# Two expert blocks taken whole ahead of the register loads, and the end of the mix and the router taken token tile by token tile

## The chip, the cores and the metric

The kernel runs on one core of a Trainium2 chip. The metric is device time in microseconds (us), the median of several runs. Weights and activations are float32; TensorE multiplies them with the weights split into a high and a low part.

## The reference, cut to what matters

Two layers, 256 tokens, width 1024. Each adds a mixing sum to x and then a feed-forward sum; in the second layer that is two of eight experts per token.

```python
for l in range(DEPTH):
    h = rms_norm(x, mix_norm_g[l])
    ...
    x = x + jnp.concatenate([ya, yb, yc], axis=-1) @ w_out[l]
    h = rms_norm(x, ffn_norm_g[l])
    if l % 2 == 0:
        x = x + swiglu(h, dense_w_gate[i], dense_w_up[i], dense_w_down[i])
    else:
        x = x + moe_swiglu(h, moe_router[i], moe_w_gate[i], moe_w_up[i], moe_w_down[i])

def moe_swiglu(h, router, wg, wu, wd):
    logits = (t @ router).astype(jnp.float32)
    top_v, top_i = lax.top_k(logits, TOP_K)          # 2 of 8
    gates = jax.nn.softmax(top_v, axis=-1)
    ...
    for e in range(N_EXPERTS):                       # FF width 3584
        out = out + gate_full[:, e:e + 1] * swiglu(t, wg[e], wu[e], wd[e])
```

## The kernel before, in words

`mix(0)`, a dense feed-forward, `mix(1)` and `experts()` follow each other. A tile scheduler sets the order of the instructions on each engine from the order in which they are written, their priorities and its own estimate of their times; `tc.issue_after` pins one instruction behind another.

**End of the mix.** W_out is applied in matmuls of three terms (L201 to L203: high part, low part, low part of the input). Its four sums (two token tiles t of 128 tokens, two halves) stay in PSUM (`acc`) and are added to `x` on VectorE at L452, at the end of `mix`.

**Router.** For each token tile, eight 128x128 transposes of `x` (L1142, in two groups of four), a copy of each group to `xT` by ScalarE (L1143), eight matmuls with the router's weights (L1145) and the two largest logits (L1147, L1148). Then `xn = x*gain` (L1150), its high part `xh` (L1151, ScalarE), the indices as floats `ixf` (L1154), the one-hots `best` and `sel` (L1156, L1158), and the low part `xl` (L1160): tile 0 on VectorE, tile 1 on GpSimd. Three matmuls with `sel` (L1163 to L1165) rank the tokens of each expert; `slot_e` (L1168) is each token's place, from which the gathering one-hots `pe` are made (L1196). A second chain (L1306 to L1320) sorts the experts by their number of tokens into `order`.

**Experts.** Places p = 0 to 7 stand for experts. Place 0 is expert 0, whatever the routing; for the others the expert's number is read from `order` into a register on the SP engine (L1178, a TENSOR_LOAD). A place takes its tokens in a kind: QUARTER (32 places, matmuls L1486), NARROW (64) or WIDE (128; its weights are split into `wh` by ScalarE, L196, and `wl` by VectorE, L197). An expert has 7 blocks of 512 hidden columns; a block is six loads of 1 MB (four for gate and up, j = 0 to 3, two for down, j = 4 and 5), 336 in all. The SP queue issues them (`eload`; L1114 for expert 0, L1116 for an expert in a register). There are 12 load buffers, so load n waits until load n - 12 has been read. A load is taken as two halves.

`halves()` (L1402) lists the halves in the order of use: first the gate and up loads of the two lead blocks (LEAD = 2, both of expert 0, kind QUARTER), then the first wide block W0 and so on; the down loads of the lead blocks follow W0's. `fill` (L1420) draws up to WINDOW = 10 halves ahead; `take` (L1427) hands one out. `work()` (L1546) makes the up parts of the two lead blocks (`small_up`), then loops over the wide blocks: `wide_up` (L1434), W0's extra QUARTER part (`quarter_up`, which reads the same loads again and so frees them), transposition of the activations (`small_T`: L1510, copied by ScalarE at L1513; `wide_T`: L1497, L1500), `wide_down` of the block before, and `small_down` (L1539) of the small blocks taken in the turn before. In the first turn that is the down part of the lead blocks, behind `wide_up` of W0. Gathers of tokens are L1250 (small kinds, `xgs`) and L1264 (wide), followed by small matmuls for the norm and the scatter (L1204, L1215, L1217).

Of the kernel before, what the change touches and what calls it, by code (L numbers as in the profile page):

```python
# [13 lines left out]
F32 = mybir.dt.float32  # L14
# [115 lines left out]
def trunk(ctx: ExitStack, tc: tile.TileContext, x_in, pos_in, wst, moe, pp_in, rr_in, sw_in, rt_in,  # L130
# [163 lines left out]
    def mix(l):  # L294
# [805 lines left out]
    def experts():  # L1100
# [22 lines left out]
        def sml(name, shape, dt=F32):  # L1123
# [5 lines left out]
                        P(1, "ffng")[:, :, None].to_broadcast([128, KD, NE]), op=ALU.mult)  # L1129
        xT = big.tile([128, 2, KD, 128], F32, name="xT", tag="xg", bufs=2)  # L1130
        xn = big.tile([128, 2, DM], F32, name="xn", tag="xg", bufs=2)
        xh = big.tile([128, 2, DM], F32R, name="xh", tag="xh")
        xl = big.tile([128, 2, DM], F32R, name="xl", tag="xl")
        mx = sml("mx", [128, 2, 8])
        ix = sml("ix", [128, 2, 8], U32)
        for t in range(2):
            psl = pb()
            for g in range(2):
                ps = pa()
                for k in range(4):  # L1140
                    ks = slice((4 * g + k) * 128, (4 * g + k + 1) * 128)
                    T.transpose(ps[:, k * 128:(k + 1) * 128], x[:, t, ks], ident)  # L1142
                act(xT[:, t, 4 * g:4 * g + 4, :], ps.rearrange("p (k s) -> p k s", k=4), AF.Copy)  # L1143
# [9 lines left out]
        ixf = sml("ixf", [128, 2, 2])  # L1153
        V.tensor_copy(ixf, ix[:, :, 0:2])  # L1154
# [265 lines left out]
        def fill(n=0):  # L1420
            while len(feed) < WINDOW and sum(h[0] is not None for h in feed) <= AHEAD + n:
# [123 lines left out]

        def work():  # L1546
            m, wjob = LEAD, None
            before = [(np_, ni, small_up(np_)) for np_, ni in narrows[:LEAD]]
            drain()
            ask(NARROWS[1])  # L1550
            for n in range(len(wides) + 1):
# [25 lines left out]
                for (np_, ni, _), z in zip(before, nT):  # L1577
                    kind = KINDS[np_][0]
                    if ni == 0:
                        accs[np_] = [pa()[:, 0:512 if kind == NARROW else 256]]  # L1580
                    small_down(accs[np_][0], kind, ni, z, [take()[2] for _ in range(4)])
                    if ni == NB - 1:
                        ended(np_, kind, accs[np_], np_ == NARROWS[-1])
# [80 lines left out]
        with tc.issue_after(held_v.ins), tc.issue_after(held_a.ins):  # L1664
            fill(0)
# [9 lines left out]
    mix(0)  # L1675
    nc.sync.dma_start(rt, rt_in[:, 0:64])
    if stop != "mix0":
        ffn()
        if stop != "ffn":
            mix(1)  # L1680
            if stop != "mix1":
                experts()
# [145 lines left out]
```

## Time and profile before

| | us |
|---|---|
| median of 3 runs | 1416.01 (1412.99 to 1417.02) |
| the profiled execution's own time | 1414.25 |
| its span in the trace | 1412.5 |

| engine | busy us | share of the span |
|---|---|---|
| PE (matmul) | 1330.2 | 94% |
| DVE | 715.0 | 51% |
| ACT | 629.0 | 45% |
| POOL | 77.9 | 6% |

DMA moves 422.64 MB. The page shows the span in 40 slices of 35.3 us: the `experts` part begins in the sixteenth, where the DMA moves 71 GB/s, and from the eighteenth on it moves 340 to 427 GB/s in nearly every slice. A busy share near 100% over a long span can hide short stages with another limit, so the stages are read one by one in the rows below.

### The profile page before, as it was taken

How to read it: one execution, taken by the hardware profiler on the slowest of the kernel's cores; microseconds unless marked ns; L12 is line 12 of the kernel's file. 1: busy time of each engine (PE TensorE's matmuls, PEld its weight loads, DVE VectorE, ACT ScalarE, POOL GpSimd, SP SyncE). 2: the span in 40 equal slices, each digit the busy share in tenths (PEclk: the TensorE clock that was granted, in tenths of full speed). 3: DMA queues.
4: the chain of work that ended last, by engine and by line, in shares of the span. 5: the costliest groups of instructions: out<-in, count | busy, mean ns of one | idle time of the engine just before them, and what ended most of it. 6: DMA issues, size and time to landing. Idle time of an engine off the chain costs nothing.

```text
span 1412.5 us, 24089 instructions
## 1 busy us (share of the span) xinstructions
PE 1330.2 (94%) x9860; PEld 965.4 (68%) x9860; DVE 715.0 (51%) x1052; ACT 629.0 (45%) x986; POOL 77.9 (6%) x127
## 2 busy tenths in 40 slices
PE   7989899999999898998999999999999999999986
PEld 7977678888888676765666555655766656656553
DVE  5686455445576555453335314524544446565443
ACT  7548264444575643453224313423434345444342
POOL 1250000000114111000000000000000000000000
PEclk9989999999999997999999999999999999999989
DMA  7410245555452231899999999989999999999995
GB/s 285 178 61 2 90 153 185 189 188 179 159 185 74 84 159 71 337 425 425 425 427 425 426 385 374 426 372 426 402 426 413 420 427 426 426 411 426 427 426 226
DMA packets 60438, 422.64 MB, mean 299 GB/s; under 512 B 7200, under 2 KB 8224, under 8 KB 10400
## 3 DMA queue, kind: packets, MB, share of 16 engines
q1 hardware_dynamic: 59760, 420.03, 73.1%
q8 instruction: 79, 1.29, 0.3%
q10 hardware_dynamic: 560, 1.00, 0.2%
q14 instruction: 39, 0.32, 0.1%
HBM read 419.95 MB, written 1.05 MB: 298 GB/s over the span
## 4 chain that ended last, share of the span: by engine, by line
PE 76%; DMA 10%; DVE 6%; ACT 3%; POOL 2%; issue 2%; SPq 0%; ACTq 0%; DVEq 0%; POOLq 0%
PE pb L1470 10%; DMA raw<-moe 10%; PE pb L202 8%; PE pb L201 7%; PE pb L203 7%; PE pa L1539 7%; PE pa L202 6%; PE pa L201 6%; PE pa L203 6%; PE pb L1486 4%; DVE wl L197 2%; PE pb L1250 1%; PE pa L371 1%; PE pa L373 1%; PE pa L372 1%
## 5 line engine op out<-in xcount | busy, mean ns | idle before, releaser
L197 DVE TENSOR_TENSOR wl<-raw,wh 128x1024 fp32r<-128x1024 f32 (+1 forms) x370 | 440.8, 1221 | 180.1 <-ACT wh L196 179.4
L196 ACT ACTIVATE wh<-raw 128x1024 fp32r<-128x1024 f32 (+1 forms) x370 | 380.5, 1053 | 230.8 <-PE pb L203 118.4
L202 PE MATMUL pb<-wl,xg 128*128 128x512 f32 x336 | 141.3, 420 | 13.2 <-DVE wl L197 12.4
L1470 PE MATMUL pb<-raw,xgs 128*64 128x256 f32 x1344 | 151.0, 380 | 0.0
L201 PE MATMUL pb<-wh,xg 128*128 128x512 f32 x336 | 136.7, 409 | 9.9 <-ACT wh L196 9.9
L203 PE MATMUL pb<-wh,xg 128*128 128x512 f32 x336 | 134.0, 399 | 0.0
L1470 PEld LDWEIGHTS pb<-raw,xgs 128*64 128x64 f32 x1344 | 95.0, 137 | 54.7 <-issue 9.3
L1539 PE MATMUL pa<-raw,aT 128*32 128x256 f32 (+1 forms) x1008 | 120.1, 454 | 0.0
L1486 PE MATMUL pb<-raw,xgs 128*32 128x256 f32 x1344 | 93.1, 395 | 10.1 <-DMA raw<-moe 10.1
L202 PEld LDWEIGHTS pb<-wl,xg 128*128 128x128 f32 x336 | 64.4, 192 | 41.9 <-DVE wl L197 25.9
L1473 ACT ACTIVATE a<-pb,rg 128x256 f32<-128x256 f32 x21 | 9.9, 473 | 174.9 <-PE pb L1470 174.9
L1501 DVE TENSOR_TENSOR aT<-pb,aT 128x512 fp32r<-128x512 f32 x21 | 14.5, 692 | 143.7 <-ACT aT L1500 143.7
L201 PEld LDWEIGHTS pb<-wh,xg 128*128 128x128 f32 x336 | 64.2, 191 | 32.1 <-ACT wh L196 18.2
L1539 PEld LDWEIGHTS pa<-raw,aT 128*32 128x32 f32 (+1 forms) x1008 | 42.8, 118 | 61.9 <-issue 46.2
L1486 PEld LDWEIGHTS pb<-raw,xgs 128*32 128x32 f32 x1344 | 45.2, 113 | 50.9 <-DMA raw<-moe 14.1
L202 PE MATMUL pb<-wl,hTh 128*128 128x512 f32 (+1 forms) x192 | 73.0, 380 | 0.0
L203 PEld LDWEIGHTS pb<-wh,xg 128*128 128x128 f32 x336 | 64.5, 192 | 12.1
L203 PE MATMUL pb<-wh,hTl 128*128 128x512 f32 (+1 forms) x192 | 71.6, 377 | 0.0
L202 PE MATMUL pa<-wl,aT 128*128 128x512 f32 x168 | 69.0, 411 | 0.5 <-DVE wl L197 0.5
L201 PE MATMUL pb<-wh,hTh 128*128 128x512 f32 (+1 forms) x192 | 67.5, 378 | 0.7 <-ACT hTh L284 0.7
L203 PE MATMUL pa<-wh,aT 128*128 128x512 f32 x168 | 66.5, 396 | 0.0
L1475 DVE SCALAR_TENSOR_TENSOR a<-pb,rg,a 128x256 f32<-128x256 f32 x21 | 10.2, 484 | 99.4 <-PE pb L1470 99.4
(384 smaller groups left out, 2058.0 us busy)
## 6 DMA issues: line engine op xcount, KB each, us to landing
raw<-moe SPq DMA_DIRECT2D x336, 1024.0 KB, 12.3
raw<-wst SPq DMA_DIRECT2D x54, 1024.0 KB, 4.8
raw<-wst SPq DMA_DIRECT2D x4, 832.0 KB, 5.1
area<-sw_in SPq DMA_DIRECT2D x2, 960.0 KB, 7.1
area<-sw_in SPq DMA_DIRECT2D x2, 664.0 KB, 6.2
x<-x_in SPq DMA_DIRECT2D x2, 512.0 KB, 5.1
raw<-wst SPq DMA_DIRECT2D x2, 512.0 KB, 7.0
out_dram<-x SPq DMA_DIRECT2D x8, 128.0 KB, 2.7
```

The lines of the kernel that those rows point to most:

```text
L196: act(h[:, 0:n], t[:, a:b], AF.Copy)
L197: (E or V).tensor_tensor(lo[:, 0:n], t[:, a:b], h[:, 0:n].bitcast(F32), op=ALU.subtract)
L201: T.matmul(o, lhsT=xh, rhs=wh, start=first, stop=False)
L202: T.matmul(o, lhsT=xh, rhs=wl, start=False, stop=False)
L203: T.matmul(o, lhsT=xl, rhs=wh, start=False, stop=last)
L371: T.matmul(ps, lhsT=wh[:, s_], rhs=hTh[:, k, :], start=(k == 0), stop=False)
L372: T.matmul(ps, lhsT=wh[:, s_], rhs=hTl[:, k, :], start=False, stop=False)
L373: T.matmul(ps, lhsT=wl[:, s_], rhs=hTh[:, k, :], start=False, stop=(k == KD - 1))
L1470: T.matmul(ps[HALF[hv], :], lhsT=z[:, k, :], rhs=w[:, o_:o_ + 256], start=(k == 0), stop=(k == KD - 1))
L1486: T.matmul(ps[QUART[g], :], lhsT=z[:, k, :], rhs=ws[g // 2 * 4 + k // 2][:, o_:o_ + 256], start=(k == 0), stop=(k == KD - 1))
L1501: V.tensor_tensor(z[:, :, 1, :], p3, z[:, :, 0, :].bitcast(F32), op=ALU.subtract)
L1539: T.matmul(acc[rows, :], lhsT=aT[:, f, :], rhs=ws[f][:, g * w:g * w + w], start=(i == 0 and f == 0), stop=(i == NB - 1 and f == 3))
```

## The change

It has four parts.

- `mix()` returns its sums; `add_to_x` adds them per token tile, in `experts` within the router's loop, tile 1 behind `diff(0)`, the low part `xl` of tile 0.
- The router is written tile by tile: transposes go into the PSUM pool `pb` instead of `pa`; `xn`, `xh`, `ixf` and `xl` are made per tile; `xh` of tile 1 stands behind the last `xT` copy, `xl` of tile 1 moves from GpSimd to VectorE, behind `sel`.
- `halves()` lists all 12 loads of the two lead blocks first (gate and up of both, then down of both), and the first `fill` may draw 24 halves, so that all 12 are issued before the register loads.
- `work()` takes the two lead blocks whole (up, transposition, down) before the loop over the wide blocks.

```diff
-        for t in range(2):
-            for nh in range(2):
-                s_ = slice(nh * 512, nh * 512 + 512)
-                V.tensor_tensor(x[:, t, s_], x[:, t, s_], acc[2 * t + nh], op=ALU.add)
-        tap(f"xm{l}", x)
+        return acc
+
+    def add_to_x(acc, t):
+        for nh in range(2):
+            s_ = slice(nh * 512, nh * 512 + 512)
+            V.tensor_tensor(x[:, t, s_], x[:, t, s_], acc[2 * t + nh], op=ALU.add)
...
+        def diff(t):
+            return V.tensor_tensor(xl[:, t, :], xn[:, t, :], xh[:, t, :].bitcast(F32), op=ALU.subtract)
+
+        first = None
         for t in range(2):
+            with tc.issue_after(first.ins) if t else ExitStack():
+                add_to_x(mixed, t)
             psl = pb()
             for g in range(2):
-                ps = pa()
+                ps = pb()
...
+            V.tensor_tensor(xn[:, t, :], x[:, t, :], gr, op=ALU.mult)
 
             V.max(mx[:, t, :], psl[:, 0:NE])
             V.max_index(ix[:, t, :], mx[:, t, :], psl[:, 0:NE])
-        for t in range(2):
-            V.tensor_tensor(xn[:, t, :], x[:, t, :], gr, op=ALU.mult)
-            held_a = act(xh[:, t, :], xn[:, t, :], AF.Copy)
+            V.tensor_copy(ixf[:, t, :], ix[:, t, 0:2])
+            with tc.issue_after(last_T.ins) if t else ExitStack():
+                held_a = act(xh[:, t, :], xn[:, t, :], AF.Copy)
+            if t == 0:
+                first = diff(0)
...
-        V.tensor_tensor(sel, best[:, :, 0, :], best[:, :, 1, :], op=ALU.add)
-        for t, E in enumerate((V, G)):
-            E.tensor_tensor(xl[:, t, :], xn[:, t, :], xh[:, t, :].bitcast(F32), op=ALU.subtract)
+        chosen = V.tensor_tensor(sel, best[:, :, 0, :], best[:, :, 1, :], op=ALU.add)
+        with tc.issue_after(chosen.ins):
+            diff(1)
...
         def halves():
-            m, before = LEAD, narrows[:LEAD]
-            for b in before:
-                yield from units(*b, range(4))
+            m, before = LEAD, []
+            for js in (range(4), (4, 5)):
+                for b in narrows[:LEAD]:
+                    yield from units(*b, js)
...
         def work():
-            m, wjob = LEAD, None
-            before = [(np_, ni, small_up(np_)) for np_, ni in narrows[:LEAD]]
+            m, before, wjob = LEAD, [], None
+            lead = [(np_, ni, small_up(np_)) for np_, ni in narrows[:LEAD]]
+            small_downs(lead, [small_T(a_, KINDS[np_][0], NARROW) for np_, _, a_ in lead])
             drain()
...
         with tc.issue_after(held_v.ins), tc.issue_after(held_a.ins):
-            fill(0)
+            fill(0, 12 * LEAD)
```

In the instruction streams it shows at three places. Line numbers of the changed kernel lie some lines higher than those of the kernel before.

**The SP queue where the expert loads begin.** Before: eight loads of expert 0, then the first read of `order`, and between the reads the four gate and up loads of W0, whose expert is in a register.

```order
L1114 DMA raw<-moe 128x2048 x8
L1178 TENSOR_LOAD order
L1178 ISA x2
L1116 ISA
L1116 DMA raw<-moe 128x2048
L1178 TENSOR_LOAD order
...
L1594 TENSOR_LOAD flag_i
L1594 ISA x2
L1114 DMA raw<-moe 128x2048 x12
```

After:

```order
L1115 DMA raw<-moe 128x2048 x12
L1189 TENSOR_LOAD order
L1189 ISA x2
...
L1610 TENSOR_LOAD flag_i
L1610 ISA x2
L1117 ISA
L1117 DMA raw<-moe 128x2048
...
L1115 DMA raw<-moe 128x2048 x8
```

Four more loads stand ahead of the register loads, all eight reads stand together behind them, and W0's first load is now the thirteenth load instead of the ninth, so that it needs a buffer that one of the first twelve has left.

**PE at the end of W_out and in the router.** Before, all eight transposes of tile 0 (L1142, x8 higher up in the stream) stand among the last matmuls of W_out; behind these:

```order
L202 MATMUL pa<-wl,hTh 128x512
L203 MATMUL pa<-wh,hTl 128x512
L1142 MATMUL pa<-cc,x 128x128 x4
L1145 MATMUL pb<-rtg,xT 128x8 x4
L1142 MATMUL pa<-cc,x 128x128 x4
L1145 MATMUL pb<-rtg,xT 128x8 x12
L1163 MATMUL pb<-sel,cc 128x8
```

After:

```order
L202 MATMUL pa<-wl,hTh 128x512
L203 MATMUL pa<-wh,hTl 128x512
L1154 MATMUL pb<-rtg,xT 128x8 x4
L1151 MATMUL pb<-cc,x 128x128 x4
L1154 MATMUL pb<-rtg,xT 128x8 x4
L1151 MATMUL pb<-cc,x 128x128 x4
L1154 MATMUL pb<-rtg,xT 128x8 x4
L1151 MATMUL pb<-cc,x 128x128 x4
L1154 MATMUL pb<-rtg,xT 128x8 x4
L1174 MATMUL pb<-sel,cc 128x8
```

Only four transposes stand among W_out's matmuls now; three groups stand behind it, and each group of transposes alternates with the logits of the group before.

**ACT and PE at the lead blocks.** `a` is the silu of a block, `aT` its transposed copy, `wh` a split of W0's loads. ACT before:

```order
L196 ACTIVATE wh<-raw 128x1024 x2
L1488 ACT_TABLE_LOAD
L1488 ACTIVATE a<-pb,rg 64x256 x2
L1269 ACTIVATE xg<-pb 128x256
L1272 ACTIVATE xgs<-pb 128x32
```

ACT after:

```order
L1500 ACT_TABLE_LOAD
L1500 ACTIVATE a<-pb,rg 64x256
L196 ACTIVATE wh<-raw 128x1024 x3
L1500 ACTIVATE a<-pb,rg 64x256
L196 ACTIVATE wh<-raw 128x1024
L1525 ACTIVATE aT<-pb 128x2x2x32 x2
L1280 ACTIVATE xg<-pb 128x256
```

PE before:

```order
L1486 MATMUL pb<-raw,xgs 32x256 x63
L1264 MATMUL pb<-pe,xh 128x160 x2
L1264 MATMUL pb<-pe,xl 128x160 x2
```

PE after:

```order
L1498 MATMUL pb<-raw,xgs 32x256 x63
L1522 MATMUL pb<-cc,a 128x64 x2
L1551 MATMUL pa<-raw,aT 32x256 x15
L1522 MATMUL pb<-cc,a 128x64 x2
L1551 MATMUL pa<-raw,aT 32x256
L1275 MATMUL pb<-pe,xh 128x160 x2
```

The down parts of the lead blocks (L1551) stand directly behind their up parts on PE, and on ACT their `aT` copies stand behind four splits of W0's first two loads.

## Rows read from the trace of the kernel before

**Rows 1.** Stages: us, engines' busy us (x), PEclk granted, DMA share, GB/s.

```profile
600.00:660.00 60.00, 52.80 (x555) 36.13 (x549) 23.30 (x29) 23.71 (x34) 0.00 (x0) 0.95 1.01 425
660.00:820.00 160.00, 157.95 (x1236) 100.10 (x1235) 67.30 (x78) 57.87 (x76) 0.00 (x0) 1.00 1.01 424
820.00:1010.00 190.00, 187.10 (x1190) 117.69 (x1190) 75.82 (x90) 64.68 (x83) 0.00 (x0) 1.00 0.96 399
1010.00:1260.00 250.00, 243.23 (x1469) 160.66 (x1466) 122.17 (x133) 107.41 (x131) 0.00 (x0) 1.00 1.01 419
```

**Rows 2.** The same view in short stretches around the change.

```profile
530.00:540.00 10.00, 7.01 (x38) 4.49 (x38) 5.68 (x11) 2.43 (x4) 1.54 (x2) 1.00 0.00 0
...
550.00:555.00 5.00, 2.64 (x12) 2.55 (x12) 2.78 (x11) 1.68 (x6) 2.28 (x4) 0.50 0.01 2
...
610.00:620.00 10.00, 8.34 (x40) 6.92 (x37) 6.99 (x7) 7.82 (x10) 0.00 (x0) 0.83 1.01 427
```

**Rows 3.** SP queue's waits, 400 to 720 us: total, times, longest.

```profile
SPq L1178 <- DVE oh L1320: 45.0, 1, 45.0
```

**Rows 4.** Timeline of SP: start, us, instructions.

```profile
557.34 2.74 SPq L1116 DMA_DIRECT2D raw<-moe  x4
566.84 30.48 SPq L1114 DMA_DIRECT2D raw<-moe  x12
598.39 4.71 SPq L1116 DMA_DIRECT2D raw<-moe  x6
```

**Rows 5.** Issue at 557.3 us (W0's first load): median us to landing.

```profile
raw<-moe SPq DMA_DIRECT2D x1, 1024.0 KB, 4.9
```

**Rows 6.** Issue at 598.4 us (the twenty-fifth load): median us to landing.

```profile
raw<-moe SPq DMA_DIRECT2D x1, 1024.0 KB, 12.3
```

**Rows 7.** Timeline of all engines, router: start, us, [idle before].

```profile
543.91 0.40 PE L203 MATMUL pa<-wh,hTl 128*128 128x512 f32 x1
...
545.91 0.64 PE L1142 MATMUL pa<-cc,x 128*128 128x128 f32 x4
...
546.38 3.00 PE L1145 MATMUL pb<-rtg,xT 128*128 128x8 f32 x24
547.23 0.58 ACT L1143 ACTIVATE xT<-pa 128x512 f32<-128x512 f32 x1
...
547.47 1.21 DVE L1160 TENSOR_TENSOR xl<-xn,xh 128x1024 fp32r<-128x1024 f32 x1
...
548.83 2.35 POOL L1160 TENSOR_TENSOR xl<-xn,xh 128x1024 fp32r<-128x1024 f32 x1 [14.77 <-ACT xh L1151]
...
549.78 1.42 DVE L1325 TENSOR_TENSOR e<-mx 128x4 f32<-128x4 f32 x1
...
551.31 0.20 DVE L1156 TENSOR_TENSOR best<-cc,ixf 128x32 f32<-128x32 f32 x1
...
551.77 0.59 PE L1163 MATMUL pb<-sel,cc 128*128 128x8 f32 x2 [2.39 <-DVE sel L1158]
```

**Rows 8.** Timeline of PE, lead blocks to second wide block.

```profile
562.55 1.06 PE L1486 MATMUL pb<-raw,xgs 128*32 128x256 f32 x2
...
564.07 7.93 PE L1486 MATMUL pb<-raw,xgs 128*32 128x256 f32 x126
...
576.90 0.48 PE L201 MATMUL pb<-wh,xg 128*128 128x512 f32 x1
...
592.45 3.66 PE L1486 MATMUL pb<-raw,xgs 128*32 128x256 f32 x64
...
598.44 3.59 PE L1539 MATMUL pa<-raw,aT 128*32 128x256 f32 x60
...
611.90 0.50 PE L201 MATMUL pb<-wh,xg 128*128 128x512 f32 x1 [1.66 <-ACT wh L196]
```

**Rows 9.** Timeline of ACT at the lead blocks.

```profile
562.27 2.00 ACT L196 ACTIVATE wh<-raw 128x1024 fp32r<-128x1024 f32 x2 [3.49 <-DMA raw<-moe]
564.18 0.26 ACT L1254 ACTIVATE xgs<-pb 128x128 f32<-128x128 f32 x1
```

More of the change, by code (lines that the diff above doesn't have):

```diff
@@ L1098, in trunk, with experts @@
     NB = FFE // 512
-    def experts():
+    def experts(mixed):
         late = ctx.enter_context(tc.tile_pool(name="mol", bufs=1, reuse_waits="tile"))
@@ L1129, in experts @@
                         P(1, "ffng")[:, :, None].to_broadcast([128, KD, NE]), op=ALU.mult)
+        xl = big.tile([128, 2, DM], F32R, name="xl", tag="xl")
         xT = big.tile([128, 2, KD, 128], F32, name="xT", tag="xg", bufs=2)
@@ L1132, in experts @@
         xh = big.tile([128, 2, DM], F32R, name="xh", tag="xh")
-        xl = big.tile([128, 2, DM], F32R, name="xl", tag="xl")
         mx = sml("mx", [128, 2, 8])
         ix = sml("ix", [128, 2, 8], U32)
+        ixf = sml("ixf", [128, 2, 2])
+        def diff(t):
+            return V.tensor_tensor(xl[:, t, :], xn[:, t, :], xh[:, t, :].bitcast(F32), op=ALU.subtract)
+        first = None
         for t in range(2):
+            with tc.issue_after(first.ins) if t else ExitStack():
+                add_to_x(mixed, t)
             psl = pb()
             for g in range(2):
-                ps = pa()
+                ps = pb()
                 for k in range(4):
@@ L1142, in experts @@
                     T.transpose(ps[:, k * 128:(k + 1) * 128], x[:, t, ks], ident)
[L1143 removed]
+                last_T = act(xT[:, t, 4 * g:4 * g + 4, :], ps.rearrange("p (k s) -> p k s", k=4), AF.Copy)
                 for k in range(4 * g, 4 * g + 4):
                     T.matmul(psl[:, 0:NE], lhsT=xT[:, t, k, :], rhs=rtg[:, k, :], start=(k == 0), stop=(k == KD - 1))
+            V.tensor_tensor(xn[:, t, :], x[:, t, :], gr, op=ALU.mult)
             V.max(mx[:, t, :], psl[:, 0:NE])
             V.max_index(ix[:, t, :], mx[:, t, :], psl[:, 0:NE])
[L1149 to L1151 removed]
+            V.tensor_copy(ixf[:, t, :], ix[:, t, 0:2])
[3 more added lines that the diff above has]
+                first = diff(0)
+        tap("xm1", x)
         layers.close()
[L1153 to L1154 removed]
         best, sel = sml("best", [128, 2, 2, NE]), sml("sel", [128, 2, NE])
@@ L1418, in experts, with fill @@
         supply = halves()
-        def fill(n=0):
-            while len(feed) < WINDOW and sum(h[0] is not None for h in feed) <= AHEAD + n:
+        def fill(n=0, window=WINDOW):
+            while len(feed) < window and sum(h[0] is not None for h in feed) <= AHEAD + n:
                 h = next(supply, None)
@@ L1544, in ended, with small_downs @@
             (steps.append if final else steps.appendleft)(finish(ready[p][2][KINDS[p].index(kind)], acc, final))
+        def small_downs(blocks, aTs):
+            for (p, i, _), aT in zip(blocks, aTs):
+                kind = KINDS[p][0]
+                if i == 0:
+                    accs[p] = [pa()[:, 0:512 if kind == NARROW else 256]]
+                small_down(accs[p][0], kind, i, aT, [take()[2] for _ in range(4)])
+                if i == NB - 1:
+                    ended(p, kind, accs[p], p == NARROWS[-1])
         def work():
-            m, wjob = LEAD, None
-            before = [(np_, ni, small_up(np_)) for np_, ni in narrows[:LEAD]]
+            m, before, wjob = LEAD, [], None
+            lead = [(np_, ni, small_up(np_)) for np_, ni in narrows[:LEAD]]
+            small_downs(lead, [small_T(a_, KINDS[np_][0], NARROW) for np_, _, a_ in lead])
             drain()
@@ L1575, in work @@
                             ended(p, QUARTER, [accs[p, QUARTER]])
[L1577 to L1583, printed above, removed]
+                small_downs(before, nT)
                 new = narrows[m:m + TURNS[n]] if n < len(wides) else []
@@ L1673, in store @@
         nc.sync.dma_start(out[t * 128:(t + 1) * 128, s_], x[:, t, s_])
-    mix(0)
+    mixed = mix(0)
+    for t in range(2):
+        add_to_x(mixed, t)
+    tap("xm0", x)
     nc.sync.dma_start(rt, rt_in[:, 0:64])
@@ L1679, in trunk @@
         if stop != "ffn":
-            mix(1)
+            mixed = mix(1)
             if stop != "mix1":
-                experts()
+                experts(mixed)
     if stop is not None:
```

## The prediction

> **What bounds the kernel now.** I read the windows by stage first, then SP's waits and timeline, then the timelines of PE, ACT and DVE where the change lies. Behind the lead blocks the bound changes three times. From 600 to 660 us DMA is full (425 GB/s) and PE is idle 7.2 of 60 us. From 660 to 1010 PE is busy 345 of 350 us and from 820 DMA has gaps (399 GB/s). From 1010 on DMA is nearly full again [rows 1]. Time that is won or lost ahead of 600 us therefore reaches the end only if it moves both the stream of loads and PE's place at 660 us; what moves one alone is swallowed by the other's wait.
>
> Ahead of the experts DMA is empty: it moves nothing from 530 to 540 us [rows 2]. The eight loads of the lead blocks have landed, and SP waits 45.0 us at the first register load for the sort into `order` [rows 3]; W0's four loads are issued at 557.34, right behind it [rows 4]. This is the hole that the change fills. PE meanwhile goes through the router: last matmul of W_out at 543.91, logits to 549.4, ranks from 551.77 [rows 7], up parts of the lead blocks from 562.55 to 572.0, W0 from 576.90 [rows 8]. Call S the start of the up parts, 562.55 now. The first load that needs a buffer of W0 is the twenty-fifth; it is issued at 598.39 [rows 4] and lands 12.3 us later [rows 6], at S + 48.1. It is the marker I follow.
>
> **The four loads ahead of the registers.** At 427 GB/s [rows 2] a load of 1.05 MB takes 2.46 us, so four take 9.8 us of a DMA that was idle. Their buffers come from W_out's weights, which are all split before its last matmul at 543.91 [rows 7], so they land ahead of the up parts. That is the largest gain that there can be: 9.8 us. The register loads are covered: they still stand behind `order` at 557.3, and what follows them in the queue now waits for PE anyway.
>
> **What W0's loads wait for instead.** They are the thirteenth to sixteenth loads now, and there are 12 buffers. The first of them needs a buffer that PE's up part of lead block 0 leaves. The present release of the same buffers is the issue of the twelve L1114 loads at 566.84 [rows 4], S + 4.3. So W0's loads move from 557.34, S - 5.2, to S + 4.3. On a DMA that is idle then the first lands 4.9 us later [rows 5], more with company, say S + 10; the second 2.46 later, S + 12.4.
>
> **The new stall.** PE ends the two up parts at S + 9.5 (572.0) [rows 8] and goes straight to the lead blocks' down parts, for which it needs `aT` from ACT. In the order, `aT` stands behind four splits of W0's first two loads and between them the second silu. ACT keeps to its order: `xgs` at 564.18 follows the two splits that began at 562.27 after 3.49 us of waiting for a load [rows 9]. Two splits take 2.00 us [rows 9]. The third split can start at S + 12.4 and ends at 13.4, silu and fourth split end at 14.9, `aT` at about 15.2. PE stands from about S + 9.8 to S + 15.2: 5.4 us. The Trainium skill (TensorE: Matmul & The Clock Gate, "Architectural detail: the array is 16× 32×32, not 1× 128×128") says that the queues of ScalarE and VectorE are strictly first in, first out; by it, too, the ready copy can't pass a waiting split, which speaks against this change.
>
> Then come the downs of both blocks, 3.7 us for 64 records (3.59 for 60 [rows 8]), two transpositions (0.5), the gathers and small matmuls that take 4.9 now (572.0 to 576.90 [rows 8]). W0 starts at S + 24.3 instead of S + 14.35. Of these 9.9 us, 4.2 are work that no longer comes after W0, so PE is 5.7 us behind. The cover for it is the 7.2 us that PE waits in 600 to 660 [rows 1]: just enough.
>
> **The marker after the change.** W0's wide up takes 15.55 us (576.90 to 592.45), and its quarter part, 3.66 us for four loads, frees one after 0.9 [rows 8]: S + 40.8, with SP's issue S + 41 to 42. DMA has been idle for some us by then (loads 13 to 24 were all issued by the end of the lead blocks), so the load lands 4.9 later, S + 46 to S + 47, and all that follow at 2.46 each. Now it is S + 48.1. Of the 9.8 us there remain 1 to 2 in the frame of S; the hole of DMA is moved behind the lead blocks rather than filled, because the number of buffers is the same. I take 1.2; if PE's cover runs out, it is 0, or a loss of up to 2.5.
>
> **Where S goes: the router.** Behind the last W_out matmul (ends 544.3 [rows 7]) there is one group of logits, 1.0 us, and then three rounds of transposes (0.64), copy (0.58) and logits (3.00 us for 24 records, 1.0 a group) [rows 7], 2.3 us each with the handover between. Nothing overlaps between the rounds, since PE goes by its order. Logits end at 544.3 + 1.0 + 6.9 = 552.2 instead of 549.4: 2.8 later. From 550 to 555 PE had the half clock, 0.50 [rows 2]; if it falls as early again, the PE part of the last two rounds doubles, up to 2 us more. Against it: the softmax difference `e` takes 1.42 us and ends with GpSimd's `xl` (548.83 + 2.35 = 551.18); VectorE's next comparison, on eight times the elements, takes 0.20 us [rows 7], so 1.2 us come back once GpSimd is out of the way. The Trainium skill (SBUF — State Buffer, "Who interferes with whom") says that VectorE and GpSimd share a port; the row fits, and the sum uses the row alone. The `xl` of tile 1 costs 1.21 us on VectorE [rows 7], but between `sel` and `slot_e` PE makes three pairs like the one at 551.77 (0.59 us a pair [rows 7], some 1.5 together), which hide it; without that cover 1.2. The `xl` of tile 0 ahead of tile 1's adds delays them by 1.2 to 1.8 us, while PE is at tile 0's logits until 547.7: hidden. Sum: S later by 2.8 - 1.2 = 1.6, at most 3.6; I take 2.2. Below 1 it is only if the clock stays at 1.00 and the rounds overlap.
>
> **The clock behind the stall.** The mean granted clock of 610 to 620 is 0.83 [rows 2], after PE had waited for loads; 0.17 of 10 us are lost, 1.7 us, in 3.4 us at half clock. The new stall of 5.4 us is of that kind. I put it at 0 to 2.4, and take 1.2.
>
> **Sum.** Execution of the profile 1414.25, - 1.2 (stream), + 2.2 (S), + 1.2 (clock) = 1416.4. The median of the runs, 1416.01, is 1.8 above the profiled execution, so the forecast is about 1418 us, 2 above the median.
>
> **The rivals.**
> 1. The full gain arrives. Then ACT doesn't hold `aT` back, PE meets W0 early, and the quarter part frees buffers 5 us sooner; for it speaks the empty DMA of [rows 2]; against it the order on ACT and the 12 buffers. 1414.25 - 9.8 + 2.2 + 1.8 = 1408.4; with half the gain 1413. A rule of the Trainium skill speaks for it (DMA: Bandwidth & Descriptors, "Rules for kernel authors"): issue a transfer early and wait late. It needs a free buffer at the other end, and that is where it ends here.
> 2. PE loses its cover. The stall drops the clock, PE is 5.7 + 2.4 us behind against 7.2 of cover, S is 3.6 late, and W1 starts later than its loads allow; PE is the bound from 660 on, so all of it reaches the end. It decides from the point at which stall and clock together pass 7.2 us. 1414.25 + 2.5 + 3.6 + 2.4 + 1.8 = 1424.6.
> 3. The change doesn't do what it says: the four loads are held by buffers that W_out frees late. Then W0's loads are later as well and the time is that of rival 2.
>
> **How the numbers follow.** The forecast, 1415 to 1421: 0.48. Rival 1: 0.20. Rival 2: 0.27. Rival 3: 0.05. A measurement of this kernel can tell 0.3%, 4.2 us, from no change, so "same" is 1411.8 to 1420.3. The forecast's case gives same 0.42 and slower 0.06; of rival 1's, 0.18 are faster and 0.02 same; rivals 2 and 3 give slower 0.28 and same 0.04. Faster 0.18, same 0.48, slower 0.34. The range reaches from rival 1's 1408 to rival 2's 1424.5.
>
> **What would show each step.** Right: all twelve lead loads landed ahead of the register loads; W0's first load issued about 4 us after S; a wait of PE for `aT` of 4 to 6 us ahead of the first L1551, with ACT in a split that waits for DMA; the twenty-fifth load issued about 41 us after S onto an idle DMA; logits over 2 to 5 us later. Wrong: PE without a gap between up and down parts, or a twenty-fifth load that lands before S + 44; then the gain is real and rival 1 holds. A clock of 0.50 in W0 points to rival 2.

## The result, and the profile after

The changed kernel takes 1425.79 us (median of 9 runs, 1419.22 to 1431.52) against 1416.01 (9 runs, 1412.91 to 1418.82): the ratio is 1.0071 with a 95% interval of 1.0047 to 1.0094. It is slower, by about twice what a measurement can tell from no change. Forecast were about 1418 us, with no change the likeliest of three outcomes (0.48), and a range from 1408 to 1424.5; the time lies above both.

The single executions differ a good deal. The end of W_out, ahead of which PE's instructions stand in nearly the same order in both kernels (four of the router's transposes apart), lay between 541.8 and 552.2 us in the traces of this study. Each stage is therefore read from its own start: the end of W_out's last matmul, and S, the start of the lead blocks' up parts.

**The hole of DMA** (the answer to [rows 3] and [rows 4]). Timeline of SP in the changed kernel:

```profile
443.19 94.35 SPq L1115 DMA_DIRECT2D raw<-moe  x12
571.24 2.63 SPq L1117 DMA_DIRECT2D raw<-moe  x4
574.70 17.63 SPq L1115 DMA_DIRECT2D raw<-moe  x8
613.03 4.39 SPq L1117 DMA_DIRECT2D raw<-moe  x6
```

All twelve lead loads are issued by 537.5 us, as the change says, and W0's four leave at 571.24, S + 4.4 (S is 566.83). The twenty-fifth is issued at 613.03, S + 46.2, where it was S + 35.8, onto an idle DMA: it lands 4.8 us later, at S + 51.0 instead of S + 48.2. Some short stretches follow, with columns as in [rows 2] (the last two are the share and rate of DMA). The last two stretches show the new hole:

```profile
550.00:555.00 5.00, 4.11 (x19) 3.61 (x18) 0.29 (x2) 2.73 (x7) 0.00 (x0) 0.50 0.00 0
...
580.00:590.00 10.00, 8.47 (x54) 4.87 (x58) 3.21 (x6) 3.15 (x10) 0.00 (x0) 0.53 1.01 423
581.53:590.81 9.28, 9.28 (x62) 5.26 (x66) 1.79 (x4) 1.69 (x7) 0.00 (x0) 0.50 1.01 425
...
600.00:610.00 10.00, 10.00 (x64) 8.91 (x63) 4.00 (x7) 3.78 (x6) 0.00 (x0) 1.00 0.27 114
610.00:620.00 10.00, 10.00 (x173) 5.97 (x175) 2.59 (x6) 2.52 (x5) 0.00 (x0) 1.00 0.57 226
```

DMA moves 114 GB/s from 600 to 610 and 226 from 610 to 620, where the kernel before kept it full ([rows 2], 427). And the granted clock is 0.53 from 580 to 590, where PE makes the down parts: 0.50, half, from 581.53 to 590.81, with PE busy throughout.

**PE and ACT at the lead blocks** (the answers to [rows 8] and [rows 9]). PE:

```profile
566.83 1.06 PE L1498 MATMUL pb<-raw,xgs 128*32 128x256 f32 x2
...
568.34 8.06 PE L1498 MATMUL pb<-raw,xgs 128*32 128x256 f32 x126
...
581.53 3.63 PE L1551 MATMUL pa<-raw,aT 128*32 128x256 f32 x30 [4.87 <-ACT aT L1525]
...
589.26 2.67 PE L1551 MATMUL pa<-raw,aT 128*32 128x256 f32 x32
...
595.50 0.48 PE L201 MATMUL pb<-wh,xg 128*128 128x512 f32 x1
...
611.07 2.15 PE L1498 MATMUL pb<-raw,xgs 128*32 128x256 f32 x36
...
622.42 0.50 PE L201 MATMUL pb<-wh,xg 128*128 128x512 f32 x1
```

ACT:

```profile
576.07 2.00 ACT L196 ACTIVATE wh<-raw 128x1024 fp32r<-128x1024 f32 x2 [2.57 <-DMA raw<-moe]
578.68 1.06 ACT L196 ACTIVATE wh<-raw 128x1024 fp32r<-128x1024 f32 x1 [0.60 <-DMA raw<-moe]
...
580.25 1.06 ACT L196 ACTIVATE wh<-raw 128x1024 fp32r<-128x1024 f32 x1
581.22 0.26 ACT L1525 ACTIVATE aT<-pb 128x128 f32<-128x128 f32 x1
```

The up parts end at 576.4. PE then stands 4.87 us for `aT`; ACT has split W0's first two loads in the meantime, waiting 2.57 us for the first and 0.60 for the second, and copies `aT` at 581.22, last in its row. The first down part takes 3.63 us for 30 records and the second 2.67 for 32, where 60 took 3.59 [rows 8]. W0 starts at 595.50, S + 28.7; before, S + 14.35. The second wide block starts at 622.42, S + 55.6, without any wait; before, S + 49.3, after a wait of 1.66 us for its split [rows 8].

**The router** (the answer to [rows 7]), PE and VectorE:

```profile
545.01 0.39 PE L203 MATMUL pa<-wh,hTl 128*128 128x512 f32 x1
...
545.24 0.95 PE L1154 MATMUL pb<-rtg,xT 128*128 128x8 f32 x8
...
549.60 1.69 PE L1154 MATMUL pb<-rtg,xT 128*128 128x8 f32 x8 [0.69 <-ACT xT L1152]
...
552.92 1.87 PE L1154 MATMUL pb<-rtg,xT 128*128 128x8 f32 x8 [0.69 <-ACT xT L1152]
...
555.20 0.14 DVE L1336 TENSOR_TENSOR e<-mx 128x4 f32<-128x4 f32 x1
...
556.07 0.57 PE L1174 MATMUL pb<-sel,cc 128*128 128x8 f32 x2 [1.27 <-DVE sel L1169]
```

Four rounds of logits instead of two; the third and fourth at half clock, 1.69 and 1.87 us instead of 0.95. They end at 554.8, 9.4 us behind W_out instead of 5.1. The difference `e` takes 0.14 us (1.42 before), so part comes back. S stands 21.4 us behind W_out instead of 18.25: 3.2 later.

**The stages behind** (the answer to [rows 1]):

```profile
600.00:660.00 60.00, 59.83 (x639) 43.08 (x640) 24.57 (x36) 23.63 (x35) 0.00 (x0) 1.00 0.81 340
660.00:820.00 160.00, 155.03 (x1217) 97.47 (x1209) 65.55 (x76) 59.19 (x76) 0.00 (x0) 0.99 1.01 422
820.00:1010.00 190.00, 187.01 (x1207) 117.25 (x1204) 80.67 (x95) 66.38 (x87) 0.00 (x0) 1.00 0.97 403
```

PE is busy 59.8 of 60 us from 600 to 660, where it used to wait 7.2: its cover is used up, and DMA, 340 GB/s instead of 425, now waits for the buffers that PE leaves.

The 11.5 us between the two profiled spans come out so: 1.1 ahead of the end of W_out, 3.2 from there to S, 3.9 from S to the landing of the sixtieth load (S + 138.3 against S + 134.4), 2.6 from there to the last load, 0.7 behind it.

### The profile page after: what moved, and what is told of

It reads as the page before. It is cut to its first block, busy times and chain, and to the rows that moved or that the text cites. A ratio compares the mean times of both kernels' runs of the same rounds, so it can differ in the third digit from the quotient of the medians.

```text
span 1424.0 us, 24091 instructions
## 1 busy us (share of the span) xinstructions
PE 1338.5 (94%) x9860; PEld 968.9 (68%) x9860; DVE 713.6 (50%) x1054; ACT 629.7 (44%) x986; POOL 76.2 (5%) x126
## 4 chain that ended last, share of the span: by engine, by line
PE 76%; DMA 9%; DVE 7%; ACT 4%; POOL 2%; issue 2%; SPq 0%; ACTq 0%; DVEq 0%; POOLq 0%
PE pb L1482 10%; DMA raw<-moe 8%; PE pb L202 8%; PE pa L1551 8%; PE pb L203 7%; PE pb L201 7%; PE pa L201 6%; PE pa L202 6%; PE pa L203 6%; PE pb L1498 4%; DVE wl L197 2%; PE pb L1261 1%; PE pa L371 1%; PE pa L372 1%; PE pa L373 1%
## 5 line engine op out<-in xcount | busy, mean ns | idle before, releaser
L1551 PE MATMUL pa<-raw,aT 128*32 128x256 f32 (+1 forms) x1008 | 126.0, 466 | 4.9 <-ACT aT L1525 4.9
L1551 PEld LDWEIGHTS pa<-raw,aT 128*32 128x32 f32 (+1 forms) x1008 | 43.5, 121 | 69.9 <-issue 52.2
L1487 DVE SCALAR_TENSOR_TENSOR a<-pb,rg,a 128x256 f32<-128x256 f32 x21 | 10.2, 484 | 99.0 <-PE pb L1482 99.0
## 6 DMA issues: line engine op xcount, KB each, us to landing
raw<-wst SPq DMA_DIRECT2D x4, 832.0 KB, 5.1
```

Source lines behind the costliest of these rows:

```text
L1551: T.matmul(acc[rows, :], lhsT=aT[:, f, :], rhs=ws[f][:, g * w:g * w + w], start=(i == 0 and f == 0), stop=(i == NB - 1 and f == 3))
```

## The experiments

Theory A: the time is lost behind the lead blocks (a wait for `aT`, the clock that falls with it, buffers of W0 that come free late), and the router adds 3.2 us. Theory B: the router carries the loss, and what happens behind the lead blocks comes out even. Ratios are against runs of the kernel before on the same chip (medians 1415.9 to 1419.1); groups of runs on different chips aren't compared with each other below 0.3%. All markers in this table are from the profiled execution, in us; "half clock" is the time at 0.50 between S + 6 and S + 48, summed from the granted clock of 2 us windows, and the gaps are PE's waits of more than 0.5 us, in the same stretch up to W0.

| kernel | S behind W_out | gaps | half clock | W0 | 25th load landed | 60th | last | ratio [95%] |
|---|---|---|---|---|---|---|---|---|
| before | 18.25 | 0 | 0 | S+14.4 | S+48.2 | S+134.4 | S+832.6 | |
| changed | 21.4 | 4.9 | 10.2 | S+28.7 | S+51.0 | S+138.3 | S+839.1 | 1.0071 [1.0047, 1.0094] |
| changed, again | 21.4 | 4.8 | 10.2 | S+28.6 | S+50.9 | S+138.4 | S+838.6 | 1.0031 [1.0008, 1.0054] |
| router alone | 21.6 | 0 | 1.1 | S+15.7 | S+51.1 | S+136.9 | S+835.9 | 1.0025 [1.0001, 1.0049] |
| loads and lead blocks alone | 18.3 | 3.5 | 3.4 | S+24.0 | S+46.3 | S+133.6 | S+833.1 | 0.9978 [0.9961, 0.9996] |
| one split left ahead of `aT` | 21.3 | 3.8, 1.1 | 10.2 | S+27.0 | S+51.1 | S+138.3 | S+836.8 | 1.0039 [1.0019, 1.0059] |
| all splits behind `aT` | 21.6 | 0.7, 2.2 | 10.2 | S+26.0 | S+50.1 | S+137.6 | S+837.1 | 1.0016 [0.9990, 1.0042] |
| the same, loads alone | 18.25 | 0.7, 2.2 | 6.8 | S+23.2 | S+47.4 | S+134.9 | S+832.4 | 0.9980 [0.9955, 1.0004] |
| changed, gap filled | 21.4 | 0 | 0 | S+23.6 | S+45.8 | S+133.3 | S+830.9 | 1.0021 [1.0000, 1.0041] |
| loads alone, gap filled | 18.25 | 0 | 0 | S+23.7 | S+46.0 | S+133.3 | S+832.2 | 0.9995 [0.9980, 1.0010] |
| downs late | 21.6 | 3.2, 0.8 | 10.2 | S+22.8 | S+57.9 | S+153.3 | S+850.4 | 1.0122 [1.0086, 1.0159] |
| router alone, transposes in `pa` | 18.8 | 0 | 0 | S+15.4 | S+49.1 | S+135.1 | S+832.8 | 1.0015 [0.9994, 1.0037] |
| changed, `pa`, gap filled | 18.1 | 0 | 0 | S+23.6 | S+45.9 | S+133.4 | S+833.6 | 1.0005 [0.9986, 1.0023] |
| before, router filled | 16.7 | 0 | 0 | S+14.7 | S+48.1 | S+134.0 | S+831.4 | 0.9988 [0.9971, 1.0004] |
| loads alone, both filled | 16.7 | 1.7 | 0 | S+24.7 | S+46.9 | S+134.3 | S+832.0 | 0.9987 [0.9965, 1.0009] |

**The changed kernel again**, beside a later group.

> The changed kernel once more, beside the others of this group. Both theories: 7 to 10 us above the kernel before; a gap of PE of 4 to 5.5 us ahead of the first down part, and half clock for some us behind it, for a length that differs between executions.

The markers repeat to 0.2 us up to the sixtieth load. The ratio is lower, 1.0031, and its interval just meets the first one (1.0047 to 1.0054): the median is 1424.25, near the first, but the runs of before on that chip have a median of 1419.1. By the two ratios the loss is 10 and 4.4 us; both theories expected 7 to 10 again.

**The two halves of the change alone.** The router part takes only the first hunks of the diff (end of mix, router), the other part only those of `halves`, `fill` and `work`.

> Only the end of the mix and the router are changed (tile by tile); loads and lead blocks as in the kernel before. S is the start of the lead blocks' up parts. Theory A (the loss is made behind the lead blocks; the router adds its own 3.2 us): the logits end 3 to 5 us later, S comes 2.5 to 3.5 us later against the end of W_out, the twenty-fifth load lands at S + 48 as before, and the time is 2 to 4.5 us above the kernel before (ratio 1.0015 to 1.003). Theory B (the router carries the whole loss, and what happens behind the lead blocks comes out even): 8 to 11 us above it.

> Only the loads and the lead blocks are changed; mix and router as in the kernel before. Theory A: S as before; in the scheduler's order two splits instead of four stand ahead of the first aT on ACT here, so PE waits 2 to 3.5 us between up and down parts, the clock still falls for some us, W0 starts at S + 24 to 28, the twenty-fifth load lands at S + 46 to 51; time 2 to 6 us above the kernel before. Theory B: within 2 us of the kernel before.

The router alone is 0.25% slower, about 3.5 us (0.1 to 7.0), as A has it and not B. One marker of A missed: the twenty-fifth load landed at S + 51.1 instead of S + 48, and the sixtieth 2.5 us later than before. In that trace half clock lasted to S + 6.0, where it was S + 3.2 before, and W0 started 1.4 us later. Half clock lasted about as long (to S + 5.3 to 6.1) in all five traces in which W_out ended late, with the router changed or not, and to S + 3.2 to 4.8 in the other ten, so this part belongs at least partly to the execution. How much the router costs behind S stays open. The loads and lead blocks alone are 0.2% faster, not slower; A expected 2 to 6 us more. Half of A's reason is still there: ACT and PE of that kernel,

```profile
570.60 2.00 ACT L196 ACTIVATE wh<-raw 128x1024 fp32r<-128x1024 f32 x2 [3.83 <-DMA raw<-moe]
...
573.12 0.28 ACT L1514 ACTIVATE aT<-pb 128x128 f32<-128x128 f32 x1
573.29 2.00 ACT L196 ACTIVATE wh<-raw 128x1024 fp32r<-128x1024 f32 x2
```

```profile
573.45 3.46 PE L1540 MATMUL pa<-raw,aT 128*32 128x256 f32 x32 [3.51 <-ACT aT L1514]
```

Two splits stand ahead of the first `aT` instead of four, PE waits 3.51 us instead of 4.87, and the clock is low for 3.4 us instead of 10.2. So the two halves don't simply add: with the router as changed, the scheduler puts two more splits ahead, and the wait that results is followed by three times as much half clock.

**The gap filled with work that is of no use.** The changed kernel with 20 matmuls of 128x512 between up parts and transpositions:

```diff
             lead = [(np_, ni, small_up(np_)) for np_, ni in narrows[:LEAD]]
+            ps = pb()
+            for _ in range(20):
+                T.matmul(ps, lhsT=xh[:, 0, 0:128], rhs=xh[:, 0, 0:512], start=True, stop=True)
             small_downs(lead, [small_T(a_, KINDS[np_][0], NARROW) for np_, _, a_ in lead])
```

> The changed kernel with 20 matmuls of 128x512 added on PE between the up parts of the lead blocks and their transpositions; their result is used by nothing. They fill the gap in which PE waits for aT (20 times 0.235 us is 4.7 us), and the wait itself stays. If half of the loss behind the gap is the clock (theory A), the clock stays at full from there on, the downs and gathers take 9 us instead of 14, W0 starts at S + 24 to 25.5 instead of S + 28.7, and the time is 3 to 4.5 us below the changed kernel although work was added. If the clock has no share, W0 starts at S + 28 to 29 and the time is that of the changed kernel.

PE's timeline and the windows:

```profile
578.37 4.83 PE L1572 MATMUL pb<-xh 128*128 128x512 f32 x20
583.13 0.68 PE L1522 MATMUL pb<-cc,a 64*128 64x64 f32 x4
...
584.80 3.66 PE L1551 MATMUL pa<-raw,aT 128*32 128x256 f32 x64
...
592.47 0.48 PE L201 MATMUL pb<-wh,xg 128*128 128x512 f32 x1
```

```profile
580.00:590.00 10.00, 9.98 (x105) 7.26 (x104) 5.00 (x8) 5.02 (x15) 0.00 (x0) 1.00 1.01 424
590.00:600.00 10.00, 10.00 (x65) 8.88 (x65) 5.74 (x18) 6.14 (x15) 0.00 (x0) 1.00 1.01 428
600.00:610.00 10.00, 10.00 (x84) 7.86 (x85) 3.03 (x8) 2.40 (x4) 0.00 (x0) 1.00 0.47 197
```

PE is given 4.83 us of useless work, `aT` comes no earlier, and W0 starts 5.1 us sooner, the twenty-fifth load lands 5.2 sooner, the sixtieth 5.0 sooner. The clock stays at 1.00 in 580 to 590 (0.53 in the changed kernel). That is the strongest result here: about 5 us of the loss behind the lead blocks are the clock and not the wait. Of the 10.2 us at half clock in the changed kernel, 9.3 lie behind the wait (S + 14.7 to S + 24.0); at half speed they cost half of that, an estimated 4.6 us, and the remaining 0.5 may be the order, which runs the down parts as one row (64 records in 3.66 us). The ratio, 1.0021, lies near the router's alone. The runs by themselves don't separate it from the repeated changed kernel (1.0031, on another chip), so the 5 us rest on the traces: two of the changed kernel, which agree to 0.2 us, against three with the gap filled, whose W0 starts at S + 23.6 or 23.7.

**The wait itself taken away.** First the splits were held back and put behind the `aT` copies by a pin; one split, of the second load, stayed ahead (the diff is that below without its first three lines, and with the pin around `small_downs`).

> The changed kernel with one more pin: both aT copies of the lead blocks stand on ACT ahead of all but one of the splits of W0. Theory A: the gap of PE between up and down parts falls from 4.9 to at most 1.5 us, the clock stays at full, W0 starts at S + 19 to 21 instead of S + 28.7, the twenty-fifth load is issued at S + 37 to 39 and lands at S + 42 to 44 instead of S + 51; time 6 to 10 us below the changed kernel, so about that of the kernel before or a little less, since the router stays late. Theory B: within 2 us of the changed kernel.

```profile
580.88 1.06 ACT L196 ACTIVATE wh<-raw 128x1024 fp32r<-128x1024 f32 x1 [5.03 <-DMA raw<-moe]
...
582.79 3.48 PE L1555 MATMUL pa<-raw,aT 128*32 128x256 f32 x32 [3.77 <-ACT aT L1529]
```

That one waited 5.03 us for its load, the second of W0, and PE waited 3.77 for `aT`; nothing was gained. The time is the one that B expected, but the wait was still there, so it doesn't decide between the two. Then all four went behind (the lines that set `hold` and `copied` are left out):

```diff
+                        with tc.issue_after(pin[0]) if cnt_splits[0] <= 8 else ExitStack():
+                            hl = split(r_, a_, b_, h2_p, l2_p) if own else split(r_, a_, b_)
+                        yield *hl, r_[:, a_:b_]
...
+            hold[0] = True
             lead = [(np_, ni, small_up(np_)) for np_, ni in narrows[:LEAD]]
-            small_downs(lead, [small_T(a_, KINDS[np_][0], NARROW) for np_, _, a_ in lead])
+            aTs = [small_T(a_, KINDS[np_][0], NARROW) for np_, _, a_ in lead]
+            hold[0], pin[0] = False, copied[0].ins
+            small_downs(lead, aTs)
```

> The changed kernel with all four splits of W0's first two loads pinned behind both aT copies (the pin before left one ahead, and the gap stayed at 3.8 us). Theory A: gap under 1.5 us, full clock behind it, W0 at S + 19 to 21, the twenty-fifth load landed at S + 41 to 43; time 7 to 11 us below the changed kernel, within 3 us of the kernel before. Theory B: within 2 us of the changed kernel. Rival C: W0 at S + 23 or later, 0 to 4 us below the changed kernel.

> Only the loads and the lead blocks changed (router as in the kernel before), and all four splits of W0's first two loads pinned behind both aT copies on ACT. Theory A: the gap of PE ahead of the first down part falls from 3.5 (lead part alone, two splits ahead) to under 1.5 us, full clock through the downs, W0 at S + 19 to 21, the twenty-fifth load issued at S + 36 to 38 and landed at S + 41 to 43 (before: S + 48.1); PE has less to wait for in 600 to 660; time 3 to 8 us below the kernel before. Rival C (the loads of the wide blocks need their splits on ACT early, so that holding them back costs what the gap costs): W0 at S + 23 or later, time as with the lead part alone, within 2 us of 0.998.

The kernel with the loads and lead blocks alone, PE, then ACT and VectorE:

```profile
575.20 1.93 PE L1546 MATMUL pa<-raw,aT 128*32 128x256 f32 x32 [0.65 <-ACT aT L1520]
...
583.59 0.45 PE L1264 MATMUL pb<-pe,xh 128*128 128x160 f32 x2 [2.23 <-DVE xgs L1273]
```

```profile
577.61 3.89 ACT L196 ACTIVATE wh<-raw 128x1024 fp32r<-128x1024 f32 x4
578.69 4.63 DVE L197 TENSOR_TENSOR wl<-raw,wh 128x1024 fp32r<-128x1024 f32 x4 [3.32 <-ACT wh L196]
581.39 0.37 ACT L1269 ACTIVATE xg<-pb 128x256 fp32r<-128x256 f32 x1
```

The wait for `aT` is 0.65 us, but the four splits now stand in one piece of 3.89 us on ACT ahead of the copies of W0's gathers (`xg`), and their low parts in one piece of 4.63 us on VectorE, until 583.32, ahead of the `xgs` for which PE then waits 2.23 us; the clock falls there instead. W0 starts at S + 23 and S + 26, where A expected S + 19 to 21. Rival C holds: ACT and VectorE have the same splits to make ahead of W0 whichever way they are put, and each of the orders tried left PE a gap.

**The down parts late again**, as in the kernel before, with the twelve loads still first:

```diff
             lead = [(np_, ni, small_up(np_)) for np_, ni in narrows[:LEAD]]
-            small_downs(lead, [small_T(a_, KINDS[np_][0], NARROW) for np_, _, a_ in lead])
+            held = deque([take()[2] for _ in range(4)] for _ in lead)
+            before = lead
...
-                small_downs(before, nT)
+                small_downs(before, nT, held)
```

> The changed kernel with the lead blocks' down parts put back behind W0's wide up; their four loads still stand among the first twelve and stay in their buffers until then. Theory A: no wait for aT, since PE goes from the up parts to gathers and W0; gap at most 2 us, full clock, W0 at S + 15 to 17 instead of S + 28.7; but four of the twelve buffers come free only at about S + 37, so DMA gets a hole there; time 2 to 6 us below the changed kernel and 2 to 6 above the kernel before. If the late router carries the loss instead (theory B): as the changed kernel.

```profile
582.68 2.54 SPq L1115 DMA_DIRECT2D raw<-moe  x4
615.54 4.90 SPq L1117 DMA_DIRECT2D raw<-moe  x6
```

```profile
600.00:610.00 10.00, 10.00 (x62) 8.74 (x60) 4.90 (x4) 4.48 (x6) 0.00 (x0) 1.00 0.03 14
...
630.00:640.00 10.00, 3.55 (x13) 2.13 (x14) 0.69 (x1) 0.77 (x2) 0.00 (x0) 0.50 1.01 427
```

It missed the other way: 1.2% above the kernel before. W0 starts at S + 22.8, not S + 15 to 17: PE waits 3.16 us in W0's gathers, whose copies stand behind the same splits on ACT, and the clock falls for 10.2 us. The next load waits at the head of SP's queue for 28.4 us, for a buffer that W0's quarter part leaves; DMA moves 14 GB/s in 600 to 610, and PE then is busy 3.55 of 10 us in 630 to 640, waiting for the loads. If the first twelve loads are all the lead blocks', the down parts have to come early too.

**The router's part.** The router alone, with its transposes back in `pa` (one word of the code), so that eight of them stand among W_out's matmuls again:

```diff
-                ps = pb()
+                ps = pa()
                 for k in range(4):
```

> Only mix and router changed, tile by tile, but with the router's transposes in the PSUM pool pa, as in the kernel before; in the order eight transposes of tile 0 stand among W_out's matmuls again and the logits come in two rounds instead of four. Theory A (the router's 3.2 us come from three rounds of transpose, copy and logits in a row): logits end 5 to 6.5 us behind W_out instead of 9.4, S 17 to 18.7 us behind it instead of 21.4, time within 1.5 us of the kernel before, 2 to 4 below the router part as written. If instead the low part of tile 0 ahead of tile 1's sums, or tile 1's low part on VectorE, makes the delay: S at 20 us or later.

The logits end 6.8 us behind W_out instead of 9.6 in the router alone as written, and S comes at 18.8 instead of 21.6. The rest of the router part was still there (the low part of tile 0 ahead of tile 1's sums, tile 1's on VectorE), so the rounds are the cause of 2.8 of the 3.4 us. This is read from one trace each; the ratios, 1.0015 and 1.0025, are too near to tell the two kernels apart.

**Both causes taken away**, in the changed kernel:

> The changed kernel with both causes taken away: transposes in pa, and 20 matmuls used by nothing over the gap behind the up parts. Theory A: S 17 to 18.7 us behind W_out, no half clock between S + 6 and S + 30, the twenty-fifth load landed at S + 44.5 to 46.5, the last load at S + 830 to 832; 7 to 10 us below the changed kernel, 1 to 4 us below the kernel before. If something else of the change costs (the order of the later blocks): 0 to 3 us above the kernel before.

The ratio is 1.0005: nothing of the loss is left that these runs could tell (at most 0.23%, 3.3 us), and nothing is gained, where A expected 1 to 4 us below the kernel before. The markers came as A has them up to the twenty-fifth load; the last load landed at S + 833.6, later than the expected S + 830 to 832.

**What the four loads are worth.** The loads and lead blocks alone, the gap filled with 16 matmuls:

> Only the loads and the lead blocks changed (router as in the kernel before), with 16 matmuls of 128x512 between up parts and transpositions, used by nothing, over the gap of 3.5 us. Theory A: no fall of the clock behind the up parts, W0 at S + 22 to 24, the twenty-fifth load landed at S + 44.5 to 46.5, the last load at S + 830 to 832 (before 832.6); so 1 to 3 us below the kernel before and no more: the four early loads are mostly given back, because DMA begins again only at S + 4.3 instead of S - 5.2. If the four loads were really worth their 9.8 us once the clock is out of the way: 7 us or more below.

Without any fall of the clock behind the lead blocks the ratio is 0.9995. The traces tell why. The twentieth load lands at S + 28.8 in the kernel before and at S + 28.0 with twelve loads ahead: DMA begins again at S + 4.4 instead of S - 5.2, and the 9.6 us are the four loads. The twenty-fourth lands 8 us earlier (S + 37.7 in the changed kernel, S + 45.7 before), but the twenty-fifth needs a buffer from W0, which starts 9 us later even at full clock. So the hole is moved by four loads. In the kernel before it lies between the landings of the twentieth and the twenty-first load, since that one is the first to wait for W0's quarter part (S + 28.8 to S + 37.7, 8.9 us); in the changed kernel it lies between the twenty-fourth and the twenty-fifth (S + 37.7 to S + 51.0, 13.4 us), and with the gap of the changed kernel filled it is 8.3 us long.

**The clock in the router.** The kernel before with eight useless matmuls behind the last logits, and the loads alone with those and 16 behind the up parts (`lm` is the last logits' matmul):

```diff
+        ps = pb()
+        with tc.issue_after(lm.ins):
+            for _ in range(8):
+                T.matmul(ps, lhsT=xh[:, 0, 0:128], rhs=xh[:, 0, 0:512], start=True, stop=True)
         best, sel = sml("best", [128, 2, 2, NE]), sml("sel", [128, 2, NE])
```

> The kernel before with eight matmuls of 128x512, used by nothing, behind the last logits, in the 2.4 us in which PE waits for VectorE's selection. It measures what the half clock in the router and the gathers costs by itself. If the dummies keep or bring back the full clock: half clock for less than 14 us around S instead of 18.6, S at 14 to 17.5 us behind the end of W_out instead of 18.25, time 1 to 4 us below the kernel before. If not: S at 18.3 to 20.5, time 0 to 2 us above it.

```profile
546.75 3.41 PE L1158 MATMUL pb<-xh 128*128 128x512 f32 x8
```

```profile
545.00:550.00 5.00, 5.00 (x24) 4.33 (x24) 3.52 (x11) 3.70 (x10) 3.42 (x4) 0.66 0.00 2
550.00:555.00 5.00, 4.41 (x32) 4.32 (x30) 4.02 (x23) 0.76 (x3) 0.07 (x1) 0.80 0.00 0
```

> The loads and lead blocks changed, the router as in the kernel before, with matmuls used by nothing at two places: eight behind the last logits, 16 behind the up parts (the order puts them ahead of the last eight of these). If the four early loads are worth nothing once the clock is held (theory A): S 16.5 to 17 us behind W_out, the twenty-fifth load landed at S + 45 to 47, the last at S + 830 to 832.5; time equal to the kernel before with the eight matmuls alone, 0.997 to 1.000 of the kernel before. If they are worth something: last load at S + 828 or earlier, ratio 0.995 or less. The stretch from the sixtieth to the last load takes 697.5 to 699.5 us if its differences are those of single executions.

The full clock comes back for a while (0.80 in 550 to 555, where it was 0.50 [rows 2]): half clock around S falls from 17.1 us, not the 18.6 of the expectation, to 13.7, and S stands 16.7 us behind W_out, 1.5 sooner. Both ratios, 0.9988 and 0.9987, have 1 in their intervals. With the loads changed as well nothing is added: no version beats the kernel before by the 0.3% that a measurement can tell, and the four loads bring nothing measurable even where the clock is held (0.9995, at best 0.9980 or 2.8 us). The lead part as it stands in the diff, 0.9978, is the lowest ratio, with an interval that ends at 0.9996; its profiled execution doesn't show a gain (last load S + 833.1 against S + 832.6), so it is taken as no change.

## Why the prediction was wrong

- **The four loads** land early (the twelfth 24.9 us ahead of S, which rules out the third rival), and the stream behind them is where it was by the twentieth load. Right, as is that "the hole of DMA is moved behind the lead blocks rather than filled".
- **The new stall.** Forecast 5.4 us from S + 9.8, by four splits ahead of `aT` on ACT; measured 4.87 from S + 9.8. Right in place, cause and size.
- **The clock behind the stall.** Forecast 1.2 us, at most 2.4. Measured 10.2 us at half clock, and 5 us gone when the clock is held. This is the step that failed: the price of the clock, and with it the cover below. The bound came from one row with 3.4 us at half clock [rows 2], as if each fall had that length. The downs, gathers and small matmuls took 14.0 us (581.53 to 595.50) instead of 9.1.
- **The marker.** Forecast was a release of the first buffer 0.9 us into W0's quarter part; it is 1.96 (611.07 to 613.03), and was 1.96 before as well (592.45 in [rows 8] to the issue of loads that waited for it at 594.41). The 0.9 was the share of one load, not the time to the issue. In the kernel before it is the twenty-first load that first waits for W0's quarter part, not the twenty-fifth, as the prediction has it; the twenty-fifth is the first only in the changed kernel. It left at S + 46.2 instead of S + 41 to 42: 1 us from this, the rest from the clock.
- **The cover.** "Just enough", 5.7 us against 7.2. With the clock, W0 was 14.3 us late instead of 9.9. Less the 4.2 that no longer come after W0, PE was 10.1 us behind, more than the 7.2, and the wait in 600 to 660 was gone. The second rival had this mechanism and its point of decision, with a chance of 0.27. That its time, 1424.6, is 1 us from the measured one is luck in part: it had 2.4 us for the clock, which cost about 5, and nothing for stretches in which 4.4 us lie. Its sign, a clock of 0.50 in W0, wasn't there either: half clock ended at S + 24.0, ahead of W0. The forecast took the middle of a range for the clock where the rows gave no reason for the middle.
- **The router.** Forecast 2.2 us, at most 3.6; measured 3.2, by the rounds and the half clock in the last two, less 1.3 from `e`. Right in mechanism, low in size: the clock fell at the same stage again and the upper end was the likelier.
- **The sum.** By the sum the two traces should differ by 2.2 us; they differ by 11.5. Of the 9.3 us between, 3.9 lie between S and the sixtieth load (the clock and the cover), 1.0 in the router, and 4.4 in stretches without a term: 1.1 ahead of the end of W_out, 2.6 between the sixtieth and the last load, 0.7 behind it. These 4.4 are no larger than what single executions differ by there.
- **Order on ACT, and early loads.** The Trainium skill (TensorE: Matmul & The Clock Gate, "Architectural detail: the array is 16× 32×32, not 1× 128×128") has the queue of ScalarE as strictly first in, first out. The trace agrees: the copy of `aT`, ready when the transposition ended at 576.7, waited behind the split at 580.25. The Trainium skill (DMA: Bandwidth & Descriptors, "Rules for kernel authors") counsels to issue a transfer early and to wait late. The four loads did land ahead of S, and brought nothing in time: 0.9995 with the clock held.
- **Open.** From the sixtieth to the last load the changed kernel took 700.2 and 700.8 us against 698.2, but the others lie between 697.1 and 700.2 with the same work in that stretch; a part of the change there can't be told from the single execution. Nor is it settled why the same two gaps, of 0.7 and 2.2 us, give 6.8 us of half clock in one kernel and 10.2 in another, or why a gap of 3.5 gave a third of what 4.9 gave.

## What to carry to other kernels

Loading more ahead of a wait moved nothing here, because no buffer came free earlier: follow the first load that needs a buffer from behind the moved work, and compare when DMA can go on, not how much it has done. A wait on the engine that sets the pace has a second price, the clock behind it; here it was as large as the wait, about 5 us behind 4.9, and twice the most that the trace of before had led to expect. Filling the gap with useless matmuls measures it. Where two parts of a change touch one scheduler, measure them apart and together: here +0.25% and -0.22% alone came to +0.3 to +0.7% together.

## What the runs showed of the hardware

A gap of PE of 3.5 us was followed by 3.4 us at half clock, gaps of 4.8 and 4.9 by 10.2, two gaps of 0.7 and 2.2 by 6.8 in one kernel and 10.2 in another, and one gap of 1.7 by none. PE was busy throughout the half clock behind the gap of 4.9 (9.3 of 9.3 us), and likewise from 555 to 565 us in the kernel before (10.0 of 10 us). Filled with matmuls, the same place had none, and PE gained 5 us on the same chain of waits. Eight matmuls in the router brought the full clock back for a while, in a stage that ran at half around them. And executions differ by some 10 us ahead of the experts alone, where the instructions are nearly the same: W_out ended at about 542 to 548 us in ten of the fifteen traces, at 550 to 552 in the other five. The clock goes with it: ahead of that point it stood at half for 34 to 38 us in the four traces that ended first (541.8 to 542.6) and for 48 to 61 us in the five late ones. The profiled executions of these five took 4.3 to 7.2 us more than the median of their kernel, and those four 1.1 to 5.4 us less, so that most of the spread of the runs seems to be made there.
